# The normed input kept through DRAM for the residual, written in a fixed place of ScalarE's order, and values turned over in time by two f32r products

## The chip, the cores and the metric

One core of a Trainium2 chip runs the kernel. The metric is the device time of one execution in microseconds (us), as the median of several runs. One further execution was recorded by the profiler; the rows below come from that one. The engines are named as the profile names them: PE is TensorE, DVE is VectorE, ACT is ScalarE, POOL is GpSimd, and SP issues most of the DMAs.

## What is computed

One layer of a streaming encoder on 512 positions of width 2048, everything in float32:

```python
mod = (silu(c) @ w_mod + b_mod)
shift1, scale1, gate1, shift2, scale2, gate2 = split(mod, 6)
h = rms_norm(x, norm1_w) * (1 + scale1) + shift1
q, f, i, g, z, xbc, dt = split(h @ w_in)
o_a = hgrn2_mixer(q, f, i, g, ...)     # chunked gated recurrence, 8 heads of 128
o_b = ssd_mixer(z, xbc, dt, ...)       # chunked scan, 16 heads of 64 in 4 groups
x = x + gate1 * (concat(o_a, o_b) @ w_out)
h = rms_norm(x, norm2_w) * (1 + scale2) + shift2
u_gate, u_val = split(causal_dwconv(h @ ffn_w_up))
x = x + gate2 * ((silu(u_gate) * u_val) @ ffn_w_down)
out = rms_norm(x, final_norm_w)
```

For the change, two places matter. The input `x` is used twice: normed, for the first projection, and unchanged, in the residual after `w_out`. And the HGRN recurrence runs over chunks of positions, for which the kernel needs its values `i` with their order in time reversed inside a block of 128 positions.

## The kernel before

**Products.** Every large product is made of three in f32r, a form that takes float32 data at reduced precision: each operand is split into hi (a cast) and lo (the rest, by a subtraction), and `mm3` (L167 to L170) adds hi*hi, lo*hi and hi*lo. Weights come in chunks of 128 partitions by 1024: SP loads `raw` (L148), ScalarE casts `whi` (L163), VectorE subtracts `wlo` (L164), and TensorE uses them. There are five buffers for raw, two each for hi and lo. The same five buffers carry the tiles `m` of the modulation matrix, which VectorE multiplies and adds up in `macc` (L191), in units that are spread between the chunks.

**Stages.** First x is loaded, normed and transposed: `x_rstd` and `x_norm` (L307 to L320) scale each of the four blocks of 128 positions by its reciprocal root mean square and turn it, into four tiles `xT[q]` of 128x2048 (1 MB), features in the partitions. In the same stretch the first modulation vectors are made, in eight pairs (`mod_pair`, whose m tiles are 1 MB each and have two buffers of their own, L234 and L245); after each pair `make_h1` makes two blocks of 128 features of h (L337 to L339). The projection by `w_in` runs along as the pairs arrive. Then come `v_group(0)`, the SSD and the HGRN mixing between the further chunks of w_in, the gates, `make_mix` (L852 to L866), which turns the mixed result into `mhi` and `mlo`, and the output projection (L883 to L930). After that the second norm and the two FFN products fill the second half of the span.

**The output projection.** It runs over four groups n of 512 output features. Before it, x is loaded a second time as four tiles x1 of 1 MB (L888), and 64 transposes by TensorE (`turn_x`, L902) with 16 copies by ScalarE (L904) make `x1T` of it, features in the partitions; they are drawn one by one between the products. At the end of each group the residual `x1T = acc * gate1 + x1T` is formed (L921). `turn_x1` (L910) turns the sum back later.

**The flip.** `flip_v` (L633 to L641) takes two of four 512-wide pieces of v for each of two head groups, multiplies each with a 128x128 reversal matrix on TensorE in float32 (L639), and copies the result back over v (L640).

**What sets the order.** The kernel is written as one program; a tile scheduler places each engine's instructions by their priority, and every tile is a buffer of a pool with so many buffers to a tag, so a tile that is asked for waits until an old one is done with. Large tiles share the tag "e" (13 buffers), "y" (2) and "a" (2). Each engine then runs its list strictly in order, and SP issues its DMAs in order. Small pieces of work (`waiting`, `active`, with a `yield`) are drawn into the order between the products.

Of the kernel before, what the change touches and what calls it, by code (L numbers as in the profile page):

```python
# [34 lines left out]
def hybrid_block_kernel(  # L35
# [58 lines left out]
    flip = CT([P, P], "flip")  # L94
# [131 lines left out]
    def mod_pair(j2):  # L226
# [22 lines left out]
        with tc.high_priority(offset=3000 if j2 else 0):  # L249
            ps = MIS()  # L250
            for i in range(4):
                PE.matmul(out=ps[:, i:i + 1], lhsT=acc[:, i * P:(i + 1) * P], rhs=ones[:, 0:1], start=True, stop=True)
            k = 2 * j2
            V.tensor_tensor(out=modT[:, 16 + k:18 + k], in0=ps[:, 0:2], in1=bT[:, 16 + k:18 + k], op=ALU.add)
            V.scalar_tensor_tensor(out=modT[:, 16 + k:18 + k], in0=modT[:, 16 + k:18 + k], scalar=1.0,
                                   in1=n1T[:, k:k + 2], op0=ALU.add, op1=ALU.mult)
            V.tensor_tensor(out=modT[:, k:k + 2], in0=ps[:, 2:4], in1=bT[:, k:k + 2], op=ALU.add)
            make_h1(k)
            make_h1(k + 1)

# [41 lines left out]
    xT = [E(name="xT", tag="a" if q == 3 else "e") for q in range(4)]  # L302
# [4 lines left out]
    xr = {}  # L307

    def x_rstd(t):
# [3 lines left out]
        xr[t] = r = SM(1, "rstd")  # L313
# [3 lines left out]
    def x_norm(t):  # L317
        A.activation(out=xs_[t], in_=xs_[t], func=AF.Copy, scale=xr[t])
        for q in range(4):
            transposed_one(xs_[t], xT[q], 4 * q, t, q < 3, ACC())  # L320

# [42 lines left out]
    acrow = drm.tile([16, S], F32, tag="acrow", name="acrow")  # L364
    dtt = CT([P, 64], "dtt")
# [268 lines left out]
    def flip_v(grp):  # L634

        for t in (1, 3):
            v = vtiles[grp][:, t * 512:(t + 1) * 512]
            ps = MIS()
            PE.matmul(out=ps, lhsT=flip, rhs=v, start=True, stop=True)  # L639
# [126 lines left out]
    for st, k0, k1 in SEGMENTS:  # L766
# [24 lines left out]
        if st is None:  # L791
            v_group(0)
            level_masks()
            continue
# [90 lines left out]
    x1 = []  # L885
    for t in range(NT):
        x1t = E(name="x1")
        nc.sync.dma_start(out=x1t, in_=xd[t * P:(t + 1) * P, :])  # L888
        x1.append(x1t)
# [3 lines left out]
    ssq2 = E(name="ssq2", tag="a")[:, 0:512]  # L893
# [4 lines left out]
    def turn_x(kt):  # L898

        ps = MIS()  # L900
        for t in range(NT):
            PE.transpose(out=ps[:, t * P:(t + 1) * P], in_=x1[t][:, kt * P:(kt + 1) * P], identity=ident)  # L902
            yield 0
        A.copy(out=x1f(kt), in_=ps)  # L904
# [9 lines left out]
    waiting.extend(turn_x(kt) for kt in range(KT))  # L914
    for n in range(4):
        accs = feat_group([(512 * n, 512)], [bl(i) for i in range(4)], chunk_src=wout, kts=order[::2], span=(8, 8),
                          rhs=(mhi, mlo), kk_in=True)
        with tc.high_priority(offset=2000 if n == 3 else 0):
# [168 lines left out]
```

## Time and profile before

| What | Value |
|---|---|
| median of 3 runs | 2477.04 us (2473.68 to 2478.78) |
| the profiled execution | 2476.07 us |
| its span | 2474.4 us |
| granted TensorE clock, mean | 0.994 |
| instructions in the span | 28806 |
| PE waiting for ACT's x at the start (L286), the longest sum of its waits | 16.5 us |
| read from and written to HBM | 329.72 MB and 4.23 MB |

The columns of a group of instructions are: line, engine and operation, output<-inputs, partitions x elements, count, then busy time in us, mean ns of one, and the idle time of the engine before them with what ended it. A row of a window has the window in us, its length, the busy us of PE, PEld, DVE, ACT and POOL with the number of instructions in parentheses, the granted clock of TensorE, the share of the DMA engines and GB/s. A row of the timeline has start, duration, engine, line, output<-inputs, the number of records put together, and in brackets the idle time before it. Consecutive products overlap in it, so TensorE's pace is read from the distances between starts.

### The profile page before, as it was taken

The page shows a single profiled execution, that of the slowest core. Times are in us where ns is not written, and L with a number is a line of the kernel's source. Part 1 is how long each engine was busy: PE and PEld are TensorE (multiplying, and loading weights), DVE is VectorE, ACT ScalarE, POOL GpSimd, SP SyncE. Part 2 cuts the span into 40 slices and gives each one's busy share as a digit, 9 for nine tenths or more (in the row PEclk, how much of TensorE's full clock was granted, in tenths as well). Part 3 has the DMA queues.
Part 4 walks back from the last instruction along what each step waited for, and adds up shares of the span by engine and source line. Part 5 has one row for each costly group of instructions (what it writes and reads, how often), then busy time and mean ns, then how long its engine had stood idle before and what let it go on. Part 6 is the DMA issues. An engine that isn't in the chain of part 4 may idle for free.

```text
span 2474.4 us, 28806 instructions
## 1 busy us (share of the span) xinstructions
PE 2409.5 (97%) x11071; PEld 1986.0 (80%) x11071; DVE 1488.5 (60%) x2262; ACT 786.7 (32%) x1142; POOL 33.1 (1%) x50
## 2 busy tenths in 40 slices
PE   6999999999999999999999999999999999999998
PEld 5787887888787777787888888888888888888887
DVE  6884877667766655778455453636363545454557
ACT  6334423333332322432132322222222222222333
POOL 1001000000000000000000000000000000000000
PEclk9999999999999999999999999999999999999999
DMA  9892334334555656466333232332333333323332
GB/s 296 270 294 80 111 117 130 111 107 155 164 175 189 233 186 200 128 204 221 94 99 97 94 102 94 96 100 94 100 97 94 101 95 95 101 94 99 98 128 86
DMA packets 262838, 335.85 MB, mean 136 GB/s; under 512 B 17092, under 2 KB 181524, under 8 KB 261420
## 3 DMA queue, kind: packets, MB, share of 16 engines
q1 hardware_dynamic: 259408, 327.42, 42.0%
q10 hardware_dynamic: 2988, 6.47, 0.8%
q8 instruction: 87, 1.43, 0.2%
q14 instruction: 51, 0.42, 0.1%
q0 software_dynamic: 304, 0.12, 0.0%
HBM read 329.72 MB, written 4.23 MB: 135 GB/s over the span
## 4 chain that ended last, share of the span: by engine, by line
PE 80%; DMA 8%; DVE 8%; ACT 1%; issue 1%; SPq 0%; POOL 0%; ACTq 0%; DVEq 0%; POOLq 0%
PE acc L168 26%; PE acc L170 25%; PE acc L169 25%; DMA m<-in_w_mod_dram 6%; DVE wlo L164 2%; DVE macc L191 1%; DVE macc L245 1%; DMA x<-in_x_dram 1%; DMA mm<-acrow 1%; PE mis L575 1%; ACT whi L163 1%; DMA raw<-in_w_in_dram 1%; PE mis L494 0%; PE mis L203 0%; DVE att L582 0%
## 5 line engine op out<-in xcount | busy, mean ns | idle before, releaser
L164 DVE TENSOR_TENSOR wlo<-raw,whi 128x1024 fp32r<-128x1024 f32 (+1 forms) x408 | 489.6, 1201 | 698.0 <-ACT whi L163 659.7
L163 ACT CAST whi<-raw 128x1024 fp32r<-128x1024 f32 (+2 forms) x416 | 425.1, 1022 | 1286.2 <-PE acc L169 544.8
L168 PE MATMUL acc<-hhi,whi 128*128 128x512 f32 x1920 | 769.2, 401 | 7.1 <-ACT hhi L338 2.6
L169 PE MATMUL acc<-hlo,whi 128*128 128x512 f32 x1920 | 751.3, 391 | 0.0
L170 PE MATMUL acc<-hhi,wlo 128*128 128x512 f32 x1920 | 748.3, 392 | 1.2 <-DVE wlo L164 1.1
L168 PEld LDWEIGHTS acc<-hhi,whi 128*128 128x128 f32 x1920 | 362.4, 189 | 83.8 <-ACT whi L163 5.9
L170 PEld LDWEIGHTS acc<-hhi,wlo 128*128 128x128 f32 x1920 | 361.5, 188 | 78.8 <-DVE wlo L164 2.3
L169 PEld LDWEIGHTS acc<-hlo,whi 128*128 128x128 f32 x1920 | 362.5, 189 | 69.5 <-issue 1.2
L191 DVE SCALAR_TENSOR_TENSOR macc<-m,cT,macc 128x512 f32<-128x512 f32 x240 | 179.7, 749 | 117.3 <-DMA m<-in_w_mod_dram 114.0
L168 PE MATMUL acc<-whi,act 128*128 128x512 f32 x640 | 249.0, 389 | 0.0
L169 PE MATMUL acc<-wlo,act 128*128 128x512 f32 x640 | 249.0, 389 | 0.0
L170 PE MATMUL acc<-whi,act 128*128 128x512 f32 x640 | 249.0, 389 | 0.0
L168 PE MATMUL acc<-whi,hhi 128*128 128x512 f32 x384 | 162.3, 423 | 0.0
L170 PE MATMUL acc<-whi,hlo 128*128 128x512 f32 x384 | 152.3, 397 | 0.0
L169 PE MATMUL acc<-wlo,hhi 128*128 128x512 f32 x384 | 151.7, 395 | 0.0
L170 PEld LDWEIGHTS acc<-whi,act 128*128 128x128 f32 x640 | 120.2, 188 | 25.0
L169 PEld LDWEIGHTS acc<-wlo,act 128*128 128x128 f32 x640 | 120.2, 188 | 24.9
L168 PEld LDWEIGHTS acc<-whi,act 128*128 128x128 f32 x640 | 120.2, 188 | 24.9
L999 DVE TENSOR_TENSOR g<-acc,gate 128x512 f32<-128x512 f32 x160 | 105.2, 683 | 3.9
L168 PE MATMUL acc<-mhi,whi 128*128 128x512 f32 x256 | 105.9, 414 | 0.0
L1000 DVE TENSOR_TENSOR x<-x,g 128x512 f32<-128x512 f32 x160 | 105.1, 682 | 0.0
L170 PE MATMUL acc<-mhi,wlo 128*128 128x512 f32 x256 | 101.8, 398 | 2.8 <-DVE wlo L164 2.8
(274 smaller groups left out, 2166.4 us busy)
## 6 DMA issues: line engine op xcount, KB each, us to landing
m<-in_w_mod_dram SPq DMA_DIRECT2D x192, 512.0 KB, 4.7
raw<-in_ffn_w_up_dram SPq DMA_DIRECT2D x352, 256.0 KB, 2.9
raw<-in_ffn_w_down_dram SPq DMA_DIRECT2D x88, 512.0 KB, 3.6
raw<-in_w_in_dram SPq DMA_DIRECT2D x96, 256.0 KB, 3.5
raw<-in_w_in_dram SPq DMA_DIRECT2D x48, 512.0 KB, 3.9
raw<-in_w_out_dram SPq DMA_DIRECT2D x32, 512.0 KB, 4.6
x<-in_x_dram SPq DMA_DIRECT2D x8, 1024.0 KB, 10.6
raw<-in_w_in_dram SPq DMA_DIRECT2D x64, 128.0 KB, 5.0
```

What stands on the lines that cost most here:

```text
L163: A.copy(out=h_, in_=r_)
L164: V.tensor_tensor(out=l_, in0=r_, in1=h_.bitcast(F32), op=ALU.subtract)
L168: PE.matmul(out=ps, lhsT=lh, rhs=rh, start=first, stop=False)
L169: PE.matmul(out=ps, lhsT=lh, rhs=rl, start=False, stop=False)
L170: PE.matmul(out=ps, lhsT=ll, rhs=rh, start=False, stop=last)
L191: V.scalar_tensor_tensor(out=acc, in0=last[:, k, :], scalar=cT[:, kt:kt + 1], in1=acc, op0=ALU.mult, op1=ALU.add)
L245: V.scalar_tensor_tensor(out=acc, in0=m[:, k, :], scalar=cT[:, kt:kt + 1], in1=acc, op0=ALU.mult, op1=ALU.add)
L575: PE.matmul(out=o, lhsT=kk[:, pr * P:(pr + 1) * P], rhs=halves(q, lv, True, base=pr * P, pairs=1), start=True, stop=True)
L999: V.tensor_tensor(out=m, in0=accs[t], in1=gates[5][:, cs], op=ALU.mult)
L1000: V.tensor_tensor(out=x1[t][:, cs], in0=x1[t][:, cs], in1=m, op=ALU.add)
```

## The change

The transposed and normed x is written from SBUF to DRAM (`keep`, four writes of 1 MB) as soon as it has been used for h, from ScalarE's DMA queue, with each write held at its place in ScalarE's program order: q=2 after modulation pair 5, q=3 after pair 7, q=0 and 1 after `v_group(0)`. Before the output projection it is loaded back as `x1T`, in place of x, and multiplied by the root mean square of its position: the reciprocals `xrms` are spread into a row over all partitions by four small products (`norm_row`), and VectorE multiplies each tile in two halves of 128x1024. The 64 transposes and 16 copies go. The tags of xT's buffers change places (q < 2 in "a", the others in "e"). In `flip_v`, v is split like every other operand and the reversal matrix is f32r: two f32r products take the place of one in float32.

```diff
--- before.py
+++ after.py
@@ -91,7 +91,7 @@
 
     ident = CT([P, P], "ident")
     make_identity(nc, ident)
-    flip = CT([P, P], "flip")
+    flip = CT([P, P], "flip", F32R)
     V.tensor_copy(out=flip, in_=ident[:, ::-1])
     ones = CT([P, P], "ones")
     V.memset(ones, 1.0)
@@ -257,6 +257,8 @@
             V.tensor_tensor(out=modT[:, k:k + 2], in0=ps[:, 2:4], in1=bT[:, k:k + 2], op=ALU.add)
             make_h1(k)
             make_h1(k + 1)
+        if j2 in (5, 7):
+            keep(j2 // 2)
 
     gates = {}
 
@@ -299,18 +301,19 @@
 
 
     xs_ = [E(name="x") for _ in range(NT)]
-    xT = [E(name="xT", tag="a" if q == 3 else "e") for q in range(4)]
+    xT = [E(name="xT", tag="a" if q < 2 else "e") for q in range(4)]
 
     def x_load(t):
         nc.sync.dma_start(out=xs_[t], in_=xd[t * P:(t + 1) * P, :])
 
     xr = {}
+    xrs, xrms = CT([P, NT], "xrs"), CT([P, NT], "xrms")
 
     def x_rstd(t):
         ssq = SM(1, "ssq")
         A.activation(out=xbc[t].rearrange("p b s -> p (b s)"), in_=xs_[t], func=AF.Square, accum_out=ssq)
         ms = SM(1, "ms")
-        xr[t] = r = SM(1, "rstd")
+        xr[t] = r = xrs[:, t:t + 1]
         A.activation(out=ms, in_=ssq, func=AF.Copy, scale=1.0 / D, bias=EPS)
         G.tensor_tensor(out=r, in0=ms, in1=expo[:, 0:1], op=ALU.pow)
 
@@ -318,6 +321,9 @@
         A.activation(out=xs_[t], in_=xs_[t], func=AF.Copy, scale=xr[t])
         for q in range(4):
             transposed_one(xs_[t], xT[q], 4 * q, t, q < 3, ACC())
+
+    def keep(q):
+        tc.keep_in_program_order(nc.scalar.dma_start(out=xspill[q], in_=xT[q]))
 
     hhi = [None] * KT
     hlo = [None] * KT
@@ -362,6 +368,7 @@
 
     drm = ctx.enter_context(tc.tile_pool(name="drm", bufs=1, space=bass.MemoryType.DRAM))
     acrow = drm.tile([16, S], F32, tag="acrow", name="acrow")
+    xspill = [drm.tile([P, 2048], F32, tag=f"xs{q}", name=f"xspill{q}") for q in range(4)]
     dtt = CT([P, 64], "dtt")
     dta = CT([P, 64], "dta")
     negb = CT([P, 16, 4, 2], "negb")
@@ -635,8 +642,13 @@
 
         for t in (1, 3):
             v = vtiles[grp][:, t * 512:(t + 1) * 512]
+            vh, vl = T("vh", F32R), T("vl", F32R)
+            A.copy(out=vh, in_=v)
+            V.tensor_tensor(out=vl, in0=v, in1=vh.bitcast(F32), op=ALU.subtract)
+            yield 3
             ps = MIS()
-            PE.matmul(out=ps, lhsT=flip, rhs=v, start=True, stop=True)
+            PE.matmul(out=ps, lhsT=flip, rhs=vh, start=True, stop=False)
+            PE.matmul(out=ps, lhsT=flip, rhs=vl, start=False, stop=True)
             A.copy(out=v, in_=ps)
             yield 0
 
@@ -790,6 +802,9 @@
             V.tensor_scalar(out=an, in0=an, scalar1=-1.0, scalar2=None, op0=ALU.mult)
         if st is None:
             v_group(0)
+            keep(0)
+            keep(1)
+            V.reciprocal(out=xrms, in_=xrs)
             level_masks()
             continue
         accs = [[ACC() for _ in b] for _, b in sets[st]]
@@ -882,26 +897,25 @@
     order = list(range(8, 16)) + list(range(0, 8))
     for kt in range(8):
         make_mix(kt)
-    x1 = []
-    for t in range(NT):
-        x1t = E(name="x1")
-        nc.sync.dma_start(out=x1t, in_=xd[t * P:(t + 1) * P, :])
-        x1.append(x1t)
     x1T = []
     for q in range(4):
         x1T.append(E(name="x1T", tag=("y", "y", "a", "e")[q]))
-    ssq2 = E(name="ssq2", tag="a")[:, 0:512]
+        nc.sync.dma_start(out=x1T[q], in_=xspill[q])
+    x1 = [E(name="x1") for _ in range(NT)]
+    rows2 = E(name="ssq2", tag="a")
+    ssq2, xrow = rows2[:, 0:512], rows2[:, 512:1024]
 
     def x1f(kt):
         return x1T[kt // 4][:, (kt % 4) * 512:(kt % 4 + 1) * 512]
 
-    def turn_x(kt):
+    def norm_row():
 
         ps = MIS()
         for t in range(NT):
-            PE.transpose(out=ps[:, t * P:(t + 1) * P], in_=x1[t][:, kt * P:(kt + 1) * P], identity=ident)
+            PE.matmul(out=ps[:, t * P:(t + 1) * P], lhsT=xrms[:, t:t + 1].broadcast_to([P, P]), rhs=ident,
+                      start=True, stop=True)
             yield 0
-        A.copy(out=x1f(kt), in_=ps)
+        V.tensor_copy(out=xrow, in_=ps)
 
     def turn_x1(q, t, bank):
 
@@ -911,10 +925,15 @@
             yield 0
         A.copy(out=x1[t][:, q * 512:(q + 1) * 512], in_=ps)
 
-    waiting.extend(turn_x(kt) for kt in range(KT))
+    waiting.append(norm_row())
     for n in range(4):
         accs = feat_group([(512 * n, 512)], [bl(i) for i in range(4)], chunk_src=wout, kts=order[::2], span=(8, 8),
                           rhs=(mhi, mlo), kk_in=True)
+        if n == 0:
+            drain()
+        for i in range(2):
+            xh = x1T[n].rearrange("p (i j s) -> p i j s", i=2, j=2)[:, i, :, :]
+            V.tensor_tensor(out=xh, in0=xh, in1=xrow.unsqueeze(1).broadcast_to([P, 2, 512]), op=ALU.mult)
         with tc.high_priority(offset=2000 if n == 3 else 0):
             for i in range(4):
                 kt = 4 * n + i
```

**ScalarE, about 150 us.** These are its rows around the casts of h for pair 5 (`hhi`), before and then after; `whi` are casts of weights, and `xspill` is the place in DRAM.

```order
L338 CAST hhi_1066<-hm_1259 128x512
L338 CAST hhi_1066<-hm_1263 128x512
L163 CAST whi_1339<-raw_1338 128x1024
L163 CAST whi_1371<-raw_1370 128x2x256
L163 CAST whi_1409<-raw_1408 128x1024
L163 CAST whi_1439<-raw_1438 128x1024
L163 CAST whi_1487<-raw_1486 128x1024
```

```order
L344 CAST hhi_1068<-hm_1261 128x512
L344 CAST hhi_1068<-hm_1265 128x512
L326 DMA xspill_126<-xT_117 128x2048
L163 CAST whi_1342<-raw_1341 128x1024
L163 CAST whi_1374<-raw_1373 128x2x256
L163 CAST whi_1412<-raw_1411 128x1024
L163 CAST whi_1442<-raw_1441 128x1024
L163 CAST whi_1490<-raw_1489 128x1024
```

The write of xT[2] (buffer 117) now stands directly behind pair 5's two casts, ahead of the next chunk's cast.

**SP, ahead of the output projection.** Its rows where x was loaded, before and then after; `raw` are chunks of w_out, `m` tiles of the modulation matrix, and 6549, 6551 and 6555 are x1T[0], [1] and [3].

```order
L148 DMA raw_6723<-in_w_out_dram 128x2x512
L184 DMA m_6729<-in_w_mod_dram 128x2x512
L148 DMA raw_6765<-in_w_out_dram 128x2x512
L888 DMA x_1091_6522<-in_x_dram 128x2048
L888 DMA x_1092_6524<-in_x_dram 128x2048
L888 DMA x_1093_6526<-in_x_dram 128x2048
L888 DMA x_1094_6528<-in_x_dram 128x2048
L184 DMA m_6780<-in_w_mod_dram 128x2x512
L148 DMA raw_6816<-in_w_out_dram 128x2x512
L184 DMA m_6822<-in_w_mod_dram 128x2x512
```

```order
L184 DMA m_6688<-in_w_mod_dram 128x2x512
L148 DMA raw_6716<-in_w_out_dram 128x2x512
L903 DMA x1T_6549<-xspill_124 128x2048
L903 DMA x1T_6551<-xspill_125 128x2048
L184 DMA m_6722<-in_w_mod_dram 128x2x512
L148 DMA raw_6750<-in_w_out_dram 128x2x512
L903 DMA x1T_6555<-xspill_127 128x2048
L184 DMA m_6765<-in_w_mod_dram 128x2x512
L148 DMA raw_6791<-in_w_out_dram 128x2x512
```

Instead of four loads in a row there are two, then an m and a raw, then one. The fourth, x1T[2], stands much earlier, between the w_in chunks of the stage before 650 us:

```order
L184 DMA m_5364<-in_w_mod_dram 128x2x512
L184 DMA m_5368<-in_w_mod_dram 128x2x512
L148 DMA raw_5425<-in_w_in_dram 128x2x512
L903 DMA x1T_6553<-xspill_126 128x2048
L184 DMA m_5431<-in_w_mod_dram 128x2x512
L148 DMA raw_5487<-in_w_in_dram 128x2x512
```

In the kernel before, the rows of that place are the same without the load.

**VectorE, in the output projection.** Its rows around the first chunks of w_out, before and then after. `wlo` is the low half of a chunk, and `ssq_1103` in the rows of L918 and L936 is the buffer that holds the row of root mean squares.

```order
L164 TENSOR_TENSOR wlo_6677<-raw_6675,whi_6676 128x1024
L164 TENSOR_TENSOR wlo_6725<-raw_6723,whi_6724 128x1024
L189 TENSOR_SCALAR macc_6779<-m_6780,cT 128x512
L191 SCALAR_TENSOR_TENSOR macc_6779<-m_6780,cT,macc_6779 128x512
L164 TENSOR_TENSOR wlo_6767<-raw_6765,whi_6766 128x1024
L191 SCALAR_TENSOR_TENSOR macc_6779<-m_6822,cT,macc_6779 128x512 x2
L191 SCALAR_TENSOR_TENSOR macc_6779<-m_6866,cT,macc_6779 128x512 x2
L191 SCALAR_TENSOR_TENSOR macc_6779<-m_6870,cT,macc_6779 128x512
L206 TENSOR_TENSOR modT<-mis_6773,p_295 128x4
L191 SCALAR_TENSOR_TENSOR macc_6779<-m_6870,cT,macc_6779 128x512
L164 TENSOR_TENSOR wlo_6818<-raw_6816,whi_6817 128x1024
```

```order
L918 COPY ssq_1103_6561<-mis_6579 128x512
L191 SCALAR_TENSOR_TENSOR macc_6408<-m_6722,cT,macc_6408 128x512
L936 TENSOR_TENSOR x1T_6549<-x1T_6549,ssq_1103_6561 128x1024
L164 TENSOR_TENSOR wlo_6680<-raw_6678,whi_6679 128x1024
L189 TENSOR_SCALAR macc_6764<-m_6765,cT 128x512
L936 TENSOR_TENSOR x1T_6549<-x1T_6549,ssq_1103_6561 128x1024
L191 SCALAR_TENSOR_TENSOR macc_6764<-m_6765,cT,macc_6764 128x512
L936 TENSOR_TENSOR x1T_6551<-x1T_6551,ssq_1103_6561 128x1024
L164 TENSOR_TENSOR wlo_6718<-raw_6716,whi_6717 128x1024
L191 SCALAR_TENSOR_TENSOR macc_6764<-m_6797,cT,macc_6764 128x512
L936 TENSOR_TENSOR x1T_6551<-x1T_6551,ssq_1103_6561 128x1024
L191 SCALAR_TENSOR_TENSOR macc_6764<-m_6797,cT,macc_6764 128x512
```

The copy of the row and the multiplications of x1T[0] and x1T[1] have moved in among the splits of the chunks; those of x1T[2] and x1T[3] follow in the same manner, the last behind the fourth wlo, counting the first of these rows.

## The prediction

> **What bounds the kernel now.** I read the page from the top: the busy time of each engine, the chain of work that ended last, the costliest groups. Then the stages that the change touches: the windows around them for each engine's load, the clock and the DMA share, and the timeline of TensorE there.
>
> ```profile
> PE 2409.5 (97%) x11071; PEld 1986.0 (80%) x11071; DVE 1488.5 (60%) x2262; ACT 786.7 (32%) x1142; POOL 33.1 (1%) x50
> PE 80%; DMA 8%; DVE 8%; ACT 1%; issue 1%; SPq 0%; POOL 0%; ACTq 0%; DVEq 0%; POOLq 0%
> L902 PE MATMUL mis<-ident,x 128*128 128x128 f32 x64 | 14.6, 277 | 2.4 <-DMA x<-in_x_dram 2.4
> 140.00:160.00 20.00, 20.00 (x94) 16.67 (x93) 17.73 (x29) 5.91 (x8) 0.00 (x0) 1.00 0.92 289
> 160.00:180.00 20.00, 20.00 (x94) 16.63 (x93) 17.71 (x28) 6.78 (x8) 0.00 (x0) 1.00 0.87 288
> 180.00:200.00 20.00, 17.01 (x73) 13.73 (x72) 12.18 (x18) 6.20 (x9) 6.20 (x7) 0.91 0.41 122
> 800.00:820.00 20.00, 19.03 (x107) 15.52 (x106) 19.60 (x38) 12.17 (x18) 0.00 (x0) 1.00 0.49 152
> 820.00:840.00 20.00, 17.57 (x82) 13.63 (x80) 7.36 (x10) 6.13 (x9) 0.00 (x0) 0.91 0.83 326
> 840.00:860.00 20.00, 20.00 (x104) 15.95 (x103) 10.18 (x14) 5.64 (x9) 0.00 (x0) 1.00 0.69 227
> ```
>
> The first row says that TensorE is busy for 97% of the span; the second that four fifths of the last chain is TensorE, with DMA and VectorE at 8% each. So a microsecond comes off the end if a TensorE instruction goes away, or if a wait of TensorE does; work of other engines counts only where TensorE waits for it. Of the two stages that the change touches, the first (140 to 200 us, where the modulation's weights come in) has its DMA queues nearly full, 0.92 and 0.87, and loses 3 us of TensorE after that. The second (800 to 880 us, the output projection) has full TensorE except for one hole in 820 to 840, where the granted clock falls to 0.91.
>
> **The change part by part.** The sum is made against the profiled execution's own 2476.07 us (span 2474.4 and 1.67 around it); the median of the three runs is 2477.04, 1.0 above it.
>
> *The 64 transposes of x, removed.* How much TensorE time is one of them?
>
> ```profile
> 841.06 0.39 PE L170 MATMUL acc<-mhi,wlo 128*128 128x512 f32 x1
> 841.29 0.27 PE L902 MATMUL mis<-ident,x 128*128 128x128 f32 x1
> 841.32 0.47 PE L168 MATMUL acc<-mhi,whi 128*128 128x512 f32 x1
> 841.63 0.39 PE L169 MATMUL acc<-mlo,whi 128*128 128x512 f32 x1
> 841.86 0.39 PE L170 MATMUL acc<-mhi,wlo 128*128 128x512 f32 x1
> 842.09 0.27 PE L902 MATMUL mis<-ident,x 128*128 128x128 f32 x1
> ```
>
> Instructions overlap, so I take distances between starts, not durations. From one L902 to the next, with three products between, are 0.80 us; the products alone start 0.23 apart, 0.69 for three. One transpose costs 0.11, 64 cost **7.0 us**. Their 16 ScalarE copies (L904) go too, but ScalarE is about 30% busy in 820 to 860 and nobody's wait; I count nothing.
>
> *The wait for x, removed.*
>
> ```profile
> 815.47 3.70 SPq L888 DMA_DIRECT2D x<-in_x_dram x4
> DMA to landing us min/median/max: 10.6/11.5/12.5
> 821.37 0.39 PE L169 MATMUL acc<-mlo,whi 128*128 128x512 f32 x1
> 824.19 0.41 PE L902 MATMUL mis<-ident,x 128*128 128x128 f32 x2 [2.43 <-DMA x<-in_x_dram]
> 824.36 0.47 PE L170 MATMUL acc<-mhi,wlo 128*128 128x512 f32 x1
> ...
> 825.44 0.63 PE L168 MATMUL acc<-mhi,whi 128*128 128x512 f32 x1
> 825.86 0.63 PE L169 MATMUL acc<-mlo,whi 128*128 128x512 f32 x1
> ...
> 828.42 0.51 PE L169 MATMUL acc<-mlo,whi 128*128 128x512 f32 x1
> 828.77 0.40 PE L170 MATMUL acc<-mhi,wlo 128*128 128x512 f32 x1
> ```
>
> TensorE reaches the first transpose while the 4 MB are on their way, and stands: the next product should have started at 821.60 and starts at 824.36, 2.76 late, of which the two transposes (0.22) are counted already: 2.5. Then, from 825.44 to 828.42, seven steps take 2.98 us instead of 1.61, and the eighth 0.35 instead of 0.23: the clock is halved, 1.5 more. Together **4.0 us**. In the new order TensorE touches the loaded tiles nowhere before the second transposition: they are VectorE's, and due only at the residual, after eight chunks of weights.
>
> [...]
>
> *The new work in that stage.* norm_row is four f32 products of 128x128. Nearest rows: the same form at L279, eight records (two to a product), and the transposes' 0.11.
>
> ```profile
> L279 PE MATMUL mis<-ident,rstd x8: 275/275/376, 1015.1 to 1016.0; 128*128 128x128 f32 x8
> L164 DVE TENSOR_TENSOR wlo<-raw,whi 128x1024 fp32r<-128x1024 f32 x392 | 479.0, 1222 | 696.4 <-ACT whi L163 658.1 <-DMA raw<-in_ffn_w_up_dram 16.9 <-DMA raw<-in_w_out_dram 8.9
> L191 DVE SCALAR_TENSOR_TENSOR macc<-m,cT,macc 128x512 f32<-128x512 f32 x240 | 179.7, 749 | 117.3 <-DMA m<-in_w_mod_dram 114.0
> 821.53 1.22 DVE L164 TENSOR_TENSOR wlo<-raw,whi 128x1024 fp32r<-128x1024 f32 x1
> 831.66 1.23 DVE L164 TENSOR_TENSOR wlo<-raw,whi 128x1024 fp32r<-128x1024 f32 x1 [8.91 <-DMA raw<-in_w_out_dram]
> ```
>
> Eight starts in 0.9 us are 0.13 a record, so a product is 0.25 and four are **1.0 us** (0.4 at a transpose's price, 1.2 at most). The eight multiplications by the row have the shape of wlo, 1.22 us each, 9.8 us of VectorE. This is the part I trust least: they stand between the splits that the next chunks of weights need. A chunk feeds 24 products, 24 x 0.23 = 5.5 us of TensorE. In the four chunks concerned VectorE has per chunk one wlo (1.22), two multiplications (2.44) and about three macc (2.2): 5.9. So it falls behind by 0.4 a chunk, 1.6 in all, and starts about even, since 800 to 820 shows it busy 19.60 of 20. Against that stands the lead that two buffers of hi and lo give, and the 8.91 us that VectorE idles today before the wlo at 831.66. I take **+1.0**; nothing at the lower end, and 8 at the upper, where each of four chunks is two late. The norm's reciprocal, moved early on VectorE, is four numbers wide and stands in a stretch where it waits for weights anyway: nothing.
>
> *The flips of v.*
>
> ```profile
> 439.53 0.39 PE L170 MATMUL acc<-hhi,wlo 128*128 128x512 f32 x1
> 439.76 1.02 PE L639 MATMUL mis<-v,flip 128*128 128x512 f32 x2
> 440.22 0.79 PE L168 MATMUL acc<-hhi,whi 128*128 128x512 f32 x1
> 440.85 0.39 PE L169 MATMUL acc<-hlo,whi 128*128 128x512 f32 x1
> ```
>
> An f32 flip holds TensorE from 439.76 to 440.22 and stretches the next product from 0.23 to 0.63: 0.86. Two f32r products are 2 x 0.23 = 0.46. Four flips save 4 x 0.40 = **1.6 us**. Each now needs a cast on ScalarE and a subtraction of 128x512 on VectorE first; the new order leaves over a dozen product rows between them and the flip, so I count nothing; if that cover fails, a wait of about 0.5 each eats the gain.
>
> *The writes of xT.* Four of 1 MB each are issued from ScalarE at fixed places. Three (q=3, 0, 1) fall after 195 us, where the queues are at 0.41 and lower: nothing. The write of q=2 falls right behind pair 5, here:
>
> ```profile
> 149.34 1.12 ACT L338 CAST hhi<-hm 128x512 fp32r<-128x512 f32 x2
> 174.57 1.29 DVE L339 TENSOR_TENSOR hlo<-hm,hhi 128x512 fp32r<-128x512 f32 x2
> 181.12 6.65 DMA m<-in_w_mod_dram
> 192.17 1.02 PE L252 MATMUL mis<-ones,macc 128*128 128x1 f32 x8 [2.99 <-DVE macc L245]
> ```
>
> At 150 us, into queues that move 289 GB/s at a share of 0.92, while the chain of waits leads through the loads of m (the last of 6.65 us) to the product at 192.17, for which TensorE has stood 2.99 us. 1 MB at 289 GB/s is 3.6 us; whatever the write takes from the loads arrives at that product. The ends are 0 (the tenth of the queues that is free takes it) and 3.6. I take **+2.5**, nearer the upper one because the loads come in bursts and the share is a mean.
>
> [...]
>
> *The loads back.* Three stand where x was loaded. The fourth, x1T[2], moves far ahead on SP, to the place where its buffer falls free:
>
> ```profile
> 641.03 0.37 SPq L184 DMA_DIRECT2D m<-in_w_mod_dram  x1
> 640.00:660.00 20.00, 20.00 (x109) 16.96 (x108) 12.30 (x26) 14.55 (x48) 2.64 (x2) 1.00 0.53 158
> ```
>
> 1 MB more ahead of that m. The queues are at 0.53 and TensorE misses nothing in 640 to 660, so the next weights come at most 3 us later (1 MB at 326 GB/s) and mostly not at all: **+0.5**.
>
> **The sum**: -7.0 - 4.0 + 1.0 + 1.0 - 1.6 + 2.5 + 0.5 = -7.6; 2476.1 - 7.6 = 2468.5 against the profiled execution, 2469.4 against the median. I forecast **2469**.
>
> **The rivals.**
>
> *VectorE becomes the bound of the output projection.* For it: 19.60 of 20 us busy just before, ten more microseconds put ahead of the splits, in program order, so that a multiplication which waits for its tile holds the next wlo too. Against it: only 7.36 and 10.18 of 20 busy in the two windows after. If each of the four chunks is two late, the stage gives back 8 instead of 1: 2469 + 7 = 2476, no change that can be told.
>
> *The removed wait was only the first of several.* TensorE gets to the next tight place sooner and stands there: for a raw of the weights (today's 8.91 wait of VectorE at 831.66 is for one; 3 MB of loads still go ahead of it), and at half clock after it. Then the 4.0 come back: 2473; with the modulation's m late as well, 2474. Little or no change.
>
> *Slower: the write in ScalarE's order holds a buffer.* The new hlo of pair 6 (174.57) takes the buffer that xT[2] leaves, so it must wait until the write has landed. Loads of x of that size took 10.6 to 12.5 us to land; the write is issued at about 150, so 24 us are there. If it lands only when the stretch empties, at about 185, VectorE stands 10 us with pair 7's macc behind it, and TensorE, already starved at 189, gets pair 7 that much later: +10, and 3.6 for the bandwidth, and some 3 of half clock on top. 2476.1 - 10.1 (the sum without the write) + 17 = 2483. It decides from a landing later than 174.6, twice what x took.
>
> *The change does not do what it says*: the loads back would have to wait for their writes. They are 450 us apart or more, so I give it nothing of its own.
>
> **How the numbers follow.** Forecast (2463 to 2472): 0.57. VectorE the bound, about 2476: 0.18. Next wait in its place, about 2474: 0.14. The write holds ScalarE and VectorE up, about 2483: 0.09. Something else slower: 0.02. The low end takes every unknown at its best: -7.0 - 4.0 + 0.4 - 1.6 = -12.2, 2463.9 on the profiled execution; 2463 with the median's own scatter. The high end takes in both cases near 2476 and the worst of the early load's 3: 2479. A measurement of this kernel tells about 0.2% (5 us) from no change: faster means under 2472.1, slower over 2482. Some of the middle cases end a little under 2472: faster 0.60, same 0.30, slower 0.10.
>
> **What would show it.** Right: no L902 and no hole at 821 to 824, clock 1.00 in 820 to 840, the stage of the output projection some 9 us shorter; two short flips with no wait before them; the product of pair 7 at 192 later by 2 to 3 us. Wrong: idle time of TensorE before L168 or L170 put down to wlo or whi between 825 and 850; a VectorE multiplication (L936) that waits for its DMA; an hlo at about 174 that waits for the write; m or raw later than before after 640.

## The result and the profile after

The changed kernel took 2461.98 us (median of 4 runs, 2459.69 to 2464.91) against 2477.64 of the kernel before, a ratio of 0.9945 (95% interval 0.9932 to 0.9958). That is 15.7 us less, twice the 7.6 of the prediction's sum, and 1 us under the low end of its range (by the ratio, from the 2477.04 on which the prediction stands, it is 2463.4, just inside). Its profiled execution took 2459.69 us, of which the span is 2458.0.

First the page of the changed kernel (busy time of the engines, chain of waits), then its windows in us (length, busy time of PE, PEld, DVE, ACT and POOL, granted clock, DMA share, GB/s):

```profile
PE 2396.6 (98%) x11015; PEld 1977.0 (80%) x11015; DVE 1500.1 (61%) x2276; ACT 779.9 (32%) x1130; POOL 33.6 (1%) x50
PE 76%; DVE 10%; DMA 10%; ACT 2%; issue 2%; POOL 1%; SPq 0%; ACTq 0%; DVEq 0%; POOLq 0%
140.00:160.00 20.00, 19.66 (x91) 16.07 (x90) 16.86 (x27) 6.43 (x9) 0.00 (x0) 1.00 0.98 324
160.00:180.00 20.00, 18.98 (x88) 15.32 (x87) 16.00 (x25) 6.70 (x8) 0.00 (x0) 1.00 0.88 293
180.00:200.00 20.00, 17.51 (x75) 14.21 (x74) 11.67 (x17) 5.42 (x10) 7.94 (x13) 0.91 0.46 146
800.00:820.00 20.00, 19.02 (x109) 15.56 (x108) 19.61 (x37) 11.04 (x16) 0.00 (x0) 1.00 0.86 307
820.00:840.00 20.00, 20.00 (x94) 16.67 (x93) 19.32 (x23) 3.16 (x3) 0.00 (x0) 1.00 0.72 222
840.00:860.00 20.00, 20.00 (x94) 16.24 (x93) 14.54 (x20) 7.52 (x10) 0.00 (x0) 1.00 0.69 223
```

TensorE's busy time fell by 12.9 us, less than the span (16.4). In the output projection the hole is gone: 20.00 of 20 us busy from 820 on, and the clock stays at 1.00. VectorE is busy 19.32 of 20 in 820 to 840, where it had 7.36: the multiplications fill it. In 140 to 180 the DMA rate rose from 289 and 288 to 324 and 293 GB/s.

Both kernels run the same 9840 products of L168 to L170 in the same sequence but for a dozen places before the 455th, 0.2275 us apart where nothing comes between. So I count through them: the time from one of them to a later one, less 0.2275 for each, is the excess of that stretch (all other TensorE work, holes and lower clock). Worked out so from the two traces, in us:

```
products           before   changed   what lies there
0 to 324            11.86      8.86   first modulation pairs
324 to 602          10.36     11.75   pairs 5 to 7, the write of q=2
602 to 1300         36.38     34.73   SSD mixing
1300 to 2260        77.90     78.31   the flips, HGRN mixing
2260 to 2600        15.78     15.50
2600 to 3266        30.07     17.50   make_mix's end, output projection
3266 to the last     5.55      5.00   second norm, FFN
```

The output projection is where most of the gain is, as forecast; the flips give nothing; and 3.0 us come from a stretch of which the prediction said nothing.

### The profile page after: what moved, and what is told of

The parts are those of the page before. It is cut to its first block, busy times and chain, and to the rows that moved or that the text cites. A ratio compares the mean times of both kernels' runs of the same rounds, so it can differ in the third digit from the quotient of the medians.

```text
span 2458.0 us, 28701 instructions
## 1 busy us (share of the span) xinstructions
PE 2396.6 (98%) x11015; PEld 1977.0 (80%) x11015; DVE 1500.1 (61%) x2276; ACT 779.9 (32%) x1130; POOL 33.6 (1%) x50
## 4 chain that ended last, share of the span: by engine, by line
PE 76%; DVE 10%; DMA 10%; ACT 2%; issue 2%; POOL 1%; SPq 0%; ACTq 0%; DVEq 0%; POOLq 0%
PE acc L168 24%; PE acc L170 24%; PE acc L169 24%; DMA m<-in_w_mod_dram 8%; DVE wlo L164 3%; DVE macc L191 3%; DVE macc L245 1%; PE mis L582 1%; ACT whi L163 1%; DMA mm<-acrow 0%; POOL rstd L275 0%; DMA raw<-in_ffn_w_up_dram 0%; DVE att L589 0%; PE mis L501 0%; DVE q L588 0%
## 5 line engine op out<-in xcount | busy, mean ns | idle before, releaser
L168 PE MATMUL acc<-hhi,whi 128*128 128x512 f32 x1920 | 765.9, 400 | 7.4 <-ACT whi L163 3.0
L170 PE MATMUL acc<-hhi,wlo 128*128 128x512 f32 x1920 | 746.7, 391 | 0.5 <-DVE wlo L164 0.3
L168 PEld LDWEIGHTS acc<-hhi,whi 128*128 128x128 f32 x1920 | 361.5, 188 | 84.2 <-ACT whi L163 6.6
L170 PEld LDWEIGHTS acc<-hhi,wlo 128*128 128x128 f32 x1920 | 360.4, 188 | 78.3 <-DVE wlo L164 2.2
L168 PE MATMUL acc<-whi,act 128*128 128x512 f32 x640 | 249.0, 389 | 0.0
L170 PE MATMUL acc<-whi,act 128*128 128x512 f32 x640 | 249.0, 389 | 0.0
L168 PE MATMUL acc<-whi,hhi 128*128 128x512 f32 x384 | 163.0, 425 | 0.0
L170 PE MATMUL acc<-whi,hlo 128*128 128x512 f32 x384 | 151.8, 396 | 0.0
L168 PEld LDWEIGHTS acc<-whi,act 128*128 128x128 f32 x640 | 120.1, 188 | 25.0
L170 PEld LDWEIGHTS acc<-whi,act 128*128 128x128 f32 x640 | 120.1, 188 | 24.9
L170 PE MATMUL acc<-mhi,wlo 128*128 128x512 f32 x256 | 100.8, 394 | 2.3 <-DVE wlo L164 2.2
L168 PE MATMUL acc<-mhi,whi 128*128 128x512 f32 x256 | 102.0, 398 | 0.0
```

The costliest lines, as they stand in the source:

```text
L168: PE.matmul(out=ps, lhsT=lh, rhs=rh, start=first, stop=False)
L170: PE.matmul(out=ps, lhsT=ll, rhs=rh, start=False, stop=last)
```

## Experiments

Ratios are against the kernel before, run beside each; the excess is that of the profiled execution. A half-clock stretch is a time in which the granted clock of TensorE is at one half.

### How far two executions of one program differ

**before_again** has no edit.

> The kernel before, once more, to see what two executions of one program differ by. If the half-clock stretches at 381 and 1122 us of its first profile are chance (holes of 2.08 and 2.22 us that fell badly into the clock's own windows), another profile has some of them missing or elsewhere, and the span moves by 1.7 us for each; the ratio is 1.000 within 0.001. Rival: they belong to the program, and all four return at the same places (38, 194, 381, 825, 1122).

**after_again** is the changed kernel, without an edit.

> The changed kernel once more, beside the variants. Theory: about 5 of the 15.7 us of the first comparison were chance (half-clock stretches of 1.7 us, three behind 200 us in the first profile of before and none in that of the changed kernel, and 2.6 us before 124 us, by which two profiles of before differ as well); then the ratio is about 0.9960 (10 us). Rival: the 15.7 us are the change's, ratio 0.9937, and again no half-clock stretch behind 200 us in the profile.

The kernel before against itself came to 0.9991 (0.9980 to 1.0002), 2473.19 us. The changed kernel came to 2461.05, 0.9944 (0.9932 to 0.9957): the first comparison repeats, and the theory's 0.9960 fell. But a part of it held. Here are windows with the two half-clock stretches of the first profile of before (380 and 1120 us), then two windows of its second profile:

```profile
380.00:400.00 20.00, 19.07 (x85) 15.57 (x86) 16.45 (x29) 5.76 (x8) 0.00 (x0) 0.91 0.37 106
1120.00:1140.00 20.00, 18.05 (x71) 14.41 (x72) 16.98 (x23) 4.20 (x4) 0.00 (x0) 0.91 0.94 310
```

```profile
340.00:360.00 20.00, 17.77 (x82) 14.27 (x81) 14.46 (x32) 6.54 (x10) 0.00 (x0) 0.91 0.35 107
380.00:400.00 20.00, 18.59 (x91) 14.91 (x90) 17.96 (x29) 5.30 (x8) 0.00 (x0) 1.00 0.37 107
```

The one at 380 is gone in the second, and there is one at 340; those at 38, 194 and 1122 have come back within 3 us. The second profile has the hole before the first transpose of x (2.12 us) too, but no fall of the clock behind it. And the excess from 0 to 324 is 9.29 there, against 11.86: the 3.0 us of the table were mostly chance.

Since single medians scatter so, I take all timed runs together: the 62 of the kernel before that ran beside the experiments have a mean of 2474.7 us (standard deviation 3.3), the 9 of the changed kernel 2462.2 (2.2). The gain is **12.5 us**, give or take 1.7. The clock records of the two kernels' first profiles show 1.0 and 0.5 and nothing between, so the mean clock of each run tells the time at half clock, 2 x (1 - clock) x span: 36.8 us in the mean of before, 28.4 in the changed kernel. In such a stretch products start 0.427 us apart in place of 0.2275 (825.44 to 828.42 in the kernel before), so a little under half of it is lost: half of the difference, 4.2 us (give or take 2), is the most that the lower clock can account for, one third of the gain. It is an upper bound, since this time counts stretches before the first product at 38 us too, and in the profiles it is 6.8 to 23.9 us before 46 us alone, whichever the kernel.

### The early swap of loads

**recip_only**:

```diff
+    xrs, xrms = CT([P, NT], "xrs"), CT([P, NT], "xrms")
-        xr[t] = r = SM(1, "rstd")
+        xr[t] = r = xrs[:, t:t + 1]
...
             v_group(0)
+            V.reciprocal(out=xrms, in_=xrs)
```

> The kernel before with nothing but the four-wide reciprocal on VectorE (its result unused). The scheduler moves some loads of m and raw on SP past each other before 125 us for it, though not just those that the change moves. Theory that the 3.0 us which the changed kernel gains before 124 us come from such swaps: products up to the 324th take another time than before by 1 to 3 us, ratio 0.999 (sooner) to 1.001 (later). Rival, that the 3.0 us come from the writes' or the tags' effect: nothing moves, within 0.5 us.

It took 2474.75 us (0.9998, 0.9987 to 1.0009); the excess from 0 to 324 is 10.16, between those of the two profiles of before. The changed kernel does move loads of m ahead of loads of raw on SP before 125 us, which I had not seen; that swaps of this kind carry 3 us has no support. The ten profiles with the change's early order have 8.9 to 11.7 there (mean 10.4), the four with the old or nearly the old one 9.3 to 11.9 (10.3).

### The transposes and the wait

**turns_back**, on the changed kernel (drawn in after the first group):

```diff
+    def turn_again():
+
+        ps = MIS()
+        for t in range(NT):
+            PE.transpose(out=ps[:, t * P:(t + 1) * P], in_=ident, identity=ident)
+            yield 0
+        A.copy(out=T("hm"), in_=ps)
...
         if n == 0:
             drain()
+            waiting.extend(turn_again() for _ in range(KT))
```

> The changed kernel with 64 transposes of 128x128 (of the identity, their result unused) and 16 copies put back between the products of the output projection's second and third group; no load of x and no wait for one. If a transpose costs 0.11 there, the stage is 7.0 us longer than in the changed kernel (0.9970 to 1.000 against before when that is at 0.996 or so); if the stage's other gain came from them too, up to 9. Rival: in a stage whose products are spread well they are hidden, under 4.

The excess from 2600 to 3266 is 24.10 against 17.50 and 18.34: 6.2 us for 64, 0.10 each. The 5 timed runs have a mean of 2468.2, 6.0 over the changed kernel (0.9969, 0.9956 to 0.9981). The term of the prediction, 7.0, is a little high. The spacing is that of the kernel before; here is its timeline:

```profile
873.08 0.27 PE L932 MATMUL mis<-ident 128*128 128x128 f32 x1
873.11 0.47 PE L168 MATMUL acc<-mhi,whi 128*128 128x512 f32 x1
873.42 0.39 PE L169 MATMUL acc<-mlo,whi 128*128 128x512 f32 x1
873.65 0.39 PE L170 MATMUL acc<-mhi,wlo 128*128 128x512 f32 x1
873.88 0.27 PE L932 MATMUL mis<-ident 128*128 128x128 f32 x1
```

**touch_x1T**, on the changed kernel:

```diff
+    def touch():
+
+        ps = MIS()
+        for q in (0, 1):
+            PE.transpose(out=ps[:, 0:P], in_=x1T[q][:, 0:P], identity=ident)
+            yield 0
+        A.copy(out=T("hm")[:, 0:P], in_=ps[:, 0:P])
+
     waiting.append(norm_row())
+    waiting.append(touch())
```

> The changed kernel with two transposes of the loaded x1T[0] and x1T[1] (unused) drawn in where the first transposes of x stood, between the 2741st and the 2742nd product. Theory: what the change removed there was TensorE's touch of a tile that has just been asked for; with the touch the hole comes back, 1 to 3 us before L932 put down to the DMA, with or without a half-clock stretch of 1.7 behind it; 2 to 4 us over the changed kernel. Rival: two loads of 1 MB instead of four land in time, and the two transposes cost 0.2.

The rival held: 2461.77 us (0.9950, 0.9935 to 0.9965), and TensorE does not wait at the touch. The timeline of touch_x1T on SP and TensorE, and its loads' time to landing:

```profile
801.97 0.82 SPq L903 DMA_DIRECT2D x1T<-xspill  x2
814.71 0.40 PE L169 MATMUL acc<-mlo,whi 128*128 128x512 f32 x1
814.94 0.38 PE L932 MATMUL mis<-ident,x1T 128*128 128x128 f32 x2
815.08 0.48 PE L170 MATMUL acc<-mhi,wlo 128*128 128x512 f32 x1
DMA to landing us min/median/max: 6.4/6.4/6.4
```

The two loads are issued 13.0 us before the touch. In the kernel before, the first of four loads of x was issued at 815.47, 6.3 us before TensorE stood at the first transpose (821.76), and they took 10.6 to 12.5 to land. SP held these loads back until a product of `make_mix` was done in the kernel before ("SPq L888 <- PE mis L864: 2.7, 2, 2.2") and in the changed one ("SPq L903 <- PE mis L879: 1.7, 1, 1.7"; us, times, longest), and in touch_x1T behind the same L879; measured from the same place in TensorE's order, they are issued some 7 us sooner in touch_x1T. So what removed the wait is the loads' place and number, two of 1 MB into buffers that fall free sooner, and not that TensorE no longer uses the tile. Place and number are not separated: by these figures a lead of 13.0 us would cover a landing of 12.5, and a landing of 6.4 would nearly fit a lead of 6.3.

### VectorE in the output projection

**mult_twice**, on the changed kernel:

```diff
             V.tensor_tensor(out=xh, in0=xh, in1=xrow.unsqueeze(1).broadcast_to([P, 2, 512]), op=ALU.mult)
+            V.tensor_tensor(out=xh, in0=xh, in1=xrow.unsqueeze(1).broadcast_to([P, 2, 512]), op=ALU.mult)
```

> The changed kernel with each of the eight multiplications by the row done twice: 9.8 us more of VectorE between the splits of the weights (the residual's values are then scaled twice). If VectorE is just within its time there, as the prediction feared, the splits come late: 5 to 10 us more. If it has room, as the trace of the changed kernel seems to show (no wait for wlo between 817 and 905 us), under 1.5 us.

2458.63 us (0.9926, 0.9912 to 0.9939): no slower at all. The excess from 2600 to 3266 is 15.55. VectorE's timeline in the changed kernel shows why; L936 are the multiplications:

```profile
819.96 1.22 DVE L164 TENSOR_TENSOR wlo<-raw,whi 128x1024 fp32r<-128x1024 f32 x1
821.27 0.48 DVE L189 TENSOR_SCALAR macc<-m,cT 128x512 f32<-128x512 f32 x1
821.68 1.22 DVE L936 TENSOR_TENSOR x1T<-x1T,ssq 128x1024 f32<-128x1024 f32 x1
822.81 0.74 DVE L191 SCALAR_TENSOR_TENSOR macc<-m,cT,macc 128x512 f32<-128x512 f32 x1
823.47 1.22 DVE L936 TENSOR_TENSOR x1T<-x1T,ssq 128x1024 f32<-128x1024 f32 x1
824.61 1.22 DVE L164 TENSOR_TENSOR wlo<-raw,whi 128x1024 fp32r<-128x1024 f32 x1
825.74 0.75 DVE L191 SCALAR_TENSOR_TENSOR macc<-m,cT,macc 128x512 f32<-128x512 f32 x1
```

Their starts are closer than their durations: a shape of 1.22 us is followed after 1.13 or 1.14, a macc of 0.74 after 0.66. One split, two multiplications and three macc make 5.4 us so, and not the 5.9 of the prediction, against 5.5 of TensorE. The next splits follow at 831.65, 836.11 and 843.18. The first three chunks take 5.4 us each in the mean; the fourth takes 7.1, of which VectorE waits 2.6 for m. So VectorE does not fall behind by its work. By the trace, the splits of 819.96 to 843.18 end 2.3 to 3.9 us before the first product that reads them. In mult_twice the scheduler spreads the sixteen over twice as many chunks (five chunks from 819.46 to 848.75 take 5.9 each, of which 0.5 are waits for m), and there the splits still end 1.1 us or more ahead. Why the kernel with more work is 3.7 us faster in the mean of its 5 runs than the changed kernel (give or take 2.6) stays open; one wait of 1.5 us on wlo at 917 us is absent from its profile.

### The write of q=2

**keep2_rest_late**, on the changed kernel; of its x1T[2], 120 of 128 partitions hold values of another block:

```diff
         if j2 in (5, 7):
-            keep(j2 // 2)
+        if j2 == 5:
+            tc.keep_in_program_order(nc.scalar.dma_start(out=xspill[2][0:8, :], in_=xT[2][0:8, :]))
+        if j2 == 7:
+            keep(3)
...
             keep(1)
+            tc.keep_in_program_order(nc.scalar.dma_start(out=xspill[2][8:P, :], in_=xT[1][8:P, :]))
```

> The changed kernel with a write of 64 KB instead of 1 MB behind pair 5; the rest of that block's place in DRAM is written behind the last of the writes, out of xT[1] (so these rows get another block's values). If the write of q=2 takes its place in full queues from the loads of m, as forecast with 2.5 us, the excess of TensorE between the 324th and the 602nd product (120 to 195 us; 10.4 and 11.6 in two profiles of before, 11.8 and 11.7 in two with the write) falls by 1.5 to 2.5. Rival, that the free tenth of the queues takes the write: within 0.7.

**keep2_double**, on the changed kernel:

```diff
         if j2 in (5, 7):
             keep(j2 // 2)
+        if j2 == 5:
+            tc.keep_in_program_order(nc.scalar.dma_start(out=xmore, in_=xT[2]))
```

> The changed kernel with the write of q=2 done twice behind pair 5, the second into a place of its own: 2 MB instead of 1 into the full queues. Left almost out, the write saved nothing that could be seen (excess 324 to 602: 9.4 with 64 KB, 11.8 and 9.2 with 1 MB). If the queues' free tenth takes it, 2 MB exceed what is free in 25 us: the excess rises by 1 to 4 us and the hlo of pair 6 may wait for the landing. Rival: there is room for 2 MB too, within 0.7.

Leaving the write nearly out saved nothing: 2463.65 us (0.9946, 0.9933 to 0.9958). With the write doubled, the mean of 7 runs is 3.3 us over the changed kernel (2465.99, 0.9960, 0.9947 to 0.9974); that is at the edge of the scatter (give or take 3), and its profile has six half-clock stretches of 3.4 us behind 200 us, so the 3.3 are not shown to be the write's. The excess where the products of pair 6 wait (453 to 509), and up to pair 7 (509 to 602):

```
                       453 to 509   509 to 602
before, before_again   0.76, 0.78   5.80, 7.37
keep2_rest_late        0.77         5.33
changed, after_again   2.22, 1.15   5.30, 4.74
keep2_double           3.48         4.08
```

The write does delay pair 6, by 0.4 to 1.4 us, and two writes by 2.7; but the stretch up to pair 7 behind it, 4 to 7 us in this table whatever stands before, takes the delay in. Over the whole stretch from 324 to 602 the four profiles without a write have a mean excess of 10.1 us, the eight with one write of 1 MB 10.0, and the one with two 11.4. The landing fits that. The changed kernel's writes and its hlo of pair 6, which by the prediction's reading needs the buffer:

```profile
146.06 0.35 ACTq L326 DMA_DIRECT2D xspill<-xT  x1
DMA to landing us min/median/max: 3.9/6.1/8.4
172.85 1.29 DVE L345 TENSOR_TENSOR hlo<-hm,hhi 128x512 fp32r<-128x512 f32 x2
```

The slowest of the four had landed 8.4 us after its issue, some 18 us before that hlo; the rival in which the write holds the buffer needed a landing after more than 24 us.

### The flips

**flips_only** is the kernel before with the diff's part in `flip_v` and the f32r matrix:

```diff
+            vh, vl = T("vh", F32R), T("vl", F32R)
+            A.copy(out=vh, in_=v)
+            V.tensor_tensor(out=vl, in0=v, in1=vh.bitcast(F32), op=ALU.subtract)
+            yield 3
             ps = MIS()
-            PE.matmul(out=ps, lhsT=flip, rhs=v, start=True, stop=True)
+            PE.matmul(out=ps, lhsT=flip, rhs=vh, start=True, stop=False)
+            PE.matmul(out=ps, lhsT=flip, rhs=vl, start=False, stop=True)
```

> The kernel before with the flips as two f32r products and nothing else. By the prediction's term 1.6 us less, 2476.0 against 2477.6 (ratio 0.9994), and the excess of TensorE over its weight products between 392 and 689 us falls by 1.6. Rival, from the two traces: the four flips save 1.6 where they stand, and the waits behind them in the HGRN stage give it back; the excess stays within 0.5 us and the ratio is 1.000.

**spill_f32flip** is the changed kernel with these lines, and the type of `flip`, the other way round.

> The changed kernel with the flips as they were, in float32. By the prediction's term 1.6 us more than the changed kernel: 2463.6 (ratio 0.9943 against before). Rival: the flips are worth nothing in sum, 2462 (0.9937). Either way the 3 us before 124 us, the clock at full speed after the output projection's start, and 13 us less there stay as in the changed kernel.

**spill_f32flip2** is the same again.

> The changed kernel with float32 flips, a second time, since its first 2465.9 stands 4 to 5 us over the changed kernel's 2462.0 and 2461.1, more than the flips' own stage shows. Theory: that was chance (five half-clock stretches behind 190 us in its profile, one in the changed kernel's first): now 0.9945 within 0.001 and an excess between the 1300th and 2260th product of 77 to 78. Rival: the flips are worth 4 us; 0.9960 again.

**flip_hi_only**, on the changed kernel:

```diff
-            V.tensor_tensor(out=vl, in0=v, in1=vh.bitcast(F32), op=ALU.subtract)
...
-            PE.matmul(out=ps, lhsT=flip, rhs=vh, start=True, stop=False)
-            PE.matmul(out=ps, lhsT=flip, rhs=vl, start=False, stop=True)
+            PE.matmul(out=ps, lhsT=flip, rhs=vh, start=True, stop=True)
```

> The changed kernel with the low half of the flip left out: one f32r product, no subtraction on VectorE, so the values lose precision. Four products (0.9 us of TensorE) and 2.7 us of VectorE go. Theory that the f32r flips' 1.6 us are eaten by waits behind the subtractions (idle time of TensorE between the 1300th and 2260th product 5.1 in two profiles of before, 6.0 to 6.4 in three with f32r flips): the excess there falls from 78.2 by 2 or more, to 76. Rival: the waits come from the order alone, the excess falls by 0.9 or less.

flips_only: 2471.84 us, 0.9992 (0.9981 to 1.0003). The changed kernel with f32 flips (spill_f32flip, spill_f32flip2): 2465.94 (0.9959, 0.9946 to 0.9973), then 2462.28 (0.9952, 0.9940 to 0.9964). flip_hi_only: 2463.99 (0.9956, 0.9941 to 0.9971). In the excess from 1300 to 2260 the flips do nothing: 77.3 to 79.2 with f32 (five profiles, mean 78.0), 77.6 to 79.3 with f32r (eight, mean 78.2), 77.9 with the high half alone. In their own places the four flips do save it: in the traces each takes 0.86 or 0.87 us as one f32 product, and 0.47 as two f32r products, 1.6 us for four. What they save comes back as waits; TensorE's waits in this stretch in the second profile of before, in that of flips_only and in that of the changed kernel:

```profile
PE mis L575 <- DVE att L582: 1.6, 3, 0.8
PE mis L203 <- DVE st L602: 1.5, 1, 1.5
PE mis L575 <- DVE q L567: 0.8, 1, 0.8
PE mis L617 <- DVE st L602: 0.4, 1, 0.4
```

```profile
PE mis L575 <- DVE att L582: 2.2, 3, 0.9
PE mis L575 <- DVE q L567: 1.5, 1, 1.5
PE mis L617 <- DVE st L602: 1.2, 1, 1.2
```

```profile
PE mis L582 <- DVE att L589: 2.2, 3, 0.9
PE mis L582 <- DVE q L574: 1.7, 1, 1.7
PE mis L624 <- DVE st L609: 1.3, 1, 1.3
PE mis L604 <- DVE modT L206: 0.5, 1, 0.5
```

The first three causes of the changed kernel are also in the kernel before (L582, L567 and L602 there are L589, L574 and L609 here), and each has grown by 0.6 to 0.9, while one of 1.5 on L203 is gone. The three stand in flips_only as well, which has no other part of the change; with f32 flips in the changed kernel, the wait on att is 1.1 in both profiles and the one on q is not among the listed ones. So they come with the f32r flips. Taking out the subtraction left the excess where it was (77.9; its profile has a half-clock stretch there, and the three of the eight that have one too have a mean of 78.2), and its waits on q and st are 1.8 and 1.5, so it is not the added work on VectorE. What is left is the recurrence's own chain on VectorE, which TensorE meets sooner, or the new order that the `yield 3` gives to the small pieces; no run separates these two.

By all timed runs flips_only has a mean of 2472.2 (12 runs), 2.5 under before, and the changed kernel 2462.2 against 2464.1 for both runs with f32 flips (12 runs): about 2 us each time, with some 1 us of error. The half-clock time falls there too, 30.5 against 36.8 us, and 28.4 against 30.8. Whether the flips bring that, or chance does, is not settled.

## Why the prediction was right, and where it was off

The forecast had the place and the two large terms right. That its sum of -7.6 is not further from the measured -12.5 is in part luck, since its errors cancel in part: 4.0 us of costs (1.0, 2.5 and 0.5 below) did not come, while the 1.6 of the flips did not show and the transposes and the wait brought some 1.6 less than forecast.

- *Mechanism and place*: right. The products 2600 to 3266 took 10.2 us less (mean excess 28.8 in four profiles with the old order, 18.6 in eight with the new one and at most two small products added there); forecast were 9.0.
- *Transposes, 7.0*: 6.0 to 6.2.
- *Wait for x, 4.0*: the hole was 1.9 to 3.2 us in the four profiles, without the two transposes in it, and the half clock followed in two of them (1.5 and 1.7): 3.3 in the mean. I had taken one execution's half clock as certain. The reason given, that TensorE no longer touches the tile, was not the one that counts.
- *norm_row, +1.0*: 0.8. In the changed kernel the eight records start at 816.47 and the next product at 817.28.
- *New waits behind VectorE, +1.0*: none there, and the wait of 0.8 us for modT at 887 (L910) is gone as well. The step that failed is the 5.9 a chunk, and with it "So it falls behind by 0.4 a chunk, 1.6 in all, and starts about even": it adds up durations on VectorE, though it rightly takes distances between starts on TensorE. By the starts a chunk is 5.4 us, within TensorE's 5.5, and the splits keep a lead of 2.3 us or more.
- *Flips, -1.6*: 1.6 saved in their places and given back as waits, nothing in the sum of their stage. The cover that I named held; the step that failed is that a TensorE instruction saved comes off the end, without asking which wait is next on the same chain.
- *Write, +2.5*: 0 at the end. With it the products of pair 6 come 0.4 to 1.4 us later, but the stretch up to pair 7 swallows that. The step that failed is "whatever the write takes from the loads arrives at that product". The full 3.6 us, the upper end of the prediction's estimate, is nowhere seen.
- *Early load, +0.5*: TensorE waits for no weights behind it; nothing to be seen.

The stages then make about -10; the 12.5 of all timed runs lie 2.5 beyond, which is about the scatter of the two figures (the stage's 10.2 is good to some 2 us, the 12.5 to 1.7). Less half-clock time outside the output projection would fill that gap, but the profiles do not bear it out: between 100 and 2400 us, the four with the old order have 3 to 4 half-clock stretches of 3.4 us, in the mean 3.5 (3.0 outside the projection), and the eight with the new one 1 to 7, in the mean 3.5 too (3.4 outside). The gap stays open.

## What to carry to other kernels

A wait that is seen in one profile has a price with a spread: here the hole came each time (1.9 to 3.2 us) and its half clock in two of four profiles, and where it came the hole lay otherwise to the grid of the clock's changes than where it stayed away in before_again (see below), so the same program should be profiled twice before a term is taken from such a row. A delay ahead of a longer wait on the same chain cost nothing that could be seen here (0.4 to 1.4 us at pair 6, ahead of 4 to 7 up to pair 7), so a cost is followed to the last wait behind it and not priced where it arises. And before a load is said to come too late, one looks at what holds its issue: here two loads of 1 MB, into buffers that fall free sooner, landed in 6.4 us (touch_x1T), where four took 10.6 to 12.5 (before), and needed no hiding.

## What the hardware showed that I had not expected

The length of a hole alone did not decide whether the clock fell. Here TensorE's timeline in the kernel before, and then in the changed kernel, at the same place of the program:

```profile
1121.95 0.59 PE L168 MATMUL acc<-hhi,whi 128*128 128x512 f32 x1 [2.22 <-ACT whi L163]
1122.33 0.63 PE L169 MATMUL acc<-hlo,whi 128*128 128x512 f32 x1
```

```profile
1106.41 0.50 PE L168 MATMUL acc<-hhi,whi 128*128 128x512 f32 x1 [2.44 <-ACT whi L163]
1106.74 0.39 PE L169 MATMUL acc<-hlo,whi 128*128 128x512 f32 x1
```

Behind the hole of 2.22 us the clock record stands at 0.5 from 1122.2 to 1125.6; behind the one of 2.44 it stays at 1.0. In the clock records of all profiles the stretches of half clock last 3.4 us or a multiple of it (6.8, 10.2, 13.7, 17.1), but for the last one of each span. More than that: within each of the 14 profiles all changes of the clock lie on one grid of 3.413 us. In the kernel before they come 2, 4, 48, 49, 103, 104, 233, 234, 320, 321 and 714 steps of it behind the start of the first record. They do not keep a fixed distance from the hole: the fall came 0.3 us after the end of the hole at 1121.95, and 1.1 us after the end of the one at 824.19. A window is, from here on, the time between two neighbouring lines of this grid.

The two rows fit the grid. The hole of 2.22 us lies whole in one window (1118.8 to 1122.2), the one of 2.44 is cut by a boundary, with 1.87 in one window (1102.4 to 1105.9) and the rest in the next. I added up TensorE's idle time in each full-clock window behind 60 us of all profiles: each of the 28 windows with 2.0 us or more was followed by a half-clock window. Below that it is mixed: 8 of the 45 windows with 1.5 to 1.97 us, 9 of the 117 with 0.85 to 1.5, and none with less. What decides there stays open, and so does whether the counts hold outside these profiles. The hole before the first transpose of x fits: 2.35 us in one window in the profile of the kernel before, 2.95 in recip_only, and cut into 0.9 and 1.2 in before_again, where the clock did not fall.
